# A recorded block of 7720 matmuls: the list scheduler's prices, array changes, clock, DMA rate and biases set anew

## The chip, the core and the metric

The kernel runs on one core of one Trainium2 chip. The metric is the time of one execution on the device in microseconds (us). PE is the matmul engine (TensorE), DVE, ACT and POOL are the vector, scalar and GpSimd engines, SP the queue that issues all the DMAs here.

## What is computed

One layer of a streaming encoder for 512 tokens of width 1024, in float32, with 16 learned tokens ahead of them (528 positions). Cut to what matters:

```python
u = rmsnorm(h); proj = u @ w_in                  # 1024 -> 8208 columns, cut into branches
c = c_val * sigmoid(c_gate)                      # conformer branch
c = causal_dwconv(c, 31 taps); c = silu(layernorm(c)); y_conf = c @ w_conf_out
q, k, v = silu(causal_dwconv(qkv, 4 taps))       # 8 heads of width 128; q, k normed
o = chunk_gated_delta_rule(q, k, v, g, beta)     # needs the inverse of a triangular matrix per chunk
y_dn = (rmsnorm(o) * silu(z)) @ w_dn_out
h = h + (sigmoid(gA) * y_conf + sigmoid(gB) * y_dn) @ w_out
f_gate, f_val = causal_dwconv(rmsnorm(h) @ w_up, 3 taps)   # 1024 -> 2 x 2816
out = rmsnorm(h + (silu(f_gate) * f_val) @ w_down)
```

## The kernel before, in words

**Products.** Features lie on partitions, tokens along the free dimension. A weight tile of 128 output columns (512 KB) is loaded by one DMA (`weights`), split into a rounded part `wh` (ACT) and the rest `wl` (DVE), and `gemm` multiplies it with an activation that is split in the same way: low weights by high activation, high by high, high by low. With 8 row blocks and two halves of the tokens (258 or 264 columns) that is 48 matmuls of the full 128x128 array to a tile; the text calls these **products** (`k`, `q`, `v`, `z` and `ga` are the branches of `w_in`, `cg` and `cv` the conformer's, then `y`, `wo`, `up`, `dn`).

**Small work.** The rest of PE's work uses a part of the array: the sums over partitions for the norms (`rs`: four matmuls of 128 rows and 32 columns for four groups of tokens, one on each group of 32 array columns, and all four in one PSUM bank), `ab` (32 columns of gates), the Gram matrices' corners (`ggm`, `qkm`), and the growing of the inverses from 32 to 128 rows (`gP`, `gX`: matmuls of 32x32 and 64x64, in `grow`). A stay of PE at such work, from the product before it to the product after it, is called a **visit** below. Transposes (`kt`, `vp`) are not counted as visits.

**What sets the order.** Nothing is issued directly. `record` writes the whole program down as calls (`Plan.add`), with the calls that each depends on. `Plan.price` gives each a duration. `Plan.order` then plays five engines against each other: at each step the engine that can start first takes, among its calls that are ready at that moment, the one with the lowest number. The number is the place in the program plus the biases of its stage (`BIAS`, `LNP`, `IVP`, `UP`, `WP`). `emit` hands the calls to the engines in that order, and each engine runs its own in sequence. So the numbers in the planner change no instruction; they change the order on each engine.

**What in it concerns PE.** A call that reads or adds to what another PE call wrote is ready 3 ns after it (`LAT['PE']['PE']`). For PSUM the place that a call touches is taken as its whole bank (`Vw.box`), so the four sums of one tile depend on each other in a row. In `look`, a call of the full array may not start before `drain`, which is 86 ns after the end of a small call, and `STAY` is added to its number while PE is at small work. The planner also keeps a model of PE's clock (`WIN`, `LOW`, `HIGH`).

Of the kernel before, what the change touches and what calls it, by code (L numbers as in the profile page):

```python
# [12 lines left out]
F32R = mybir.dt.float32r  # L13
# [53 lines left out]
class Vw:  # L67
    """a view of a tile: the steps to it, and the same steps taken on a stand-in to know its bounds"""
# [52 lines left out]
class Op:  # L121
    _fields = ("eng", "fn", "a", "k", "prio", "deps", "succ", "late", "wait", "cost", "ready", "end", "tiles", "lat", "table")
# [18 lines left out]
WIN = 3413.3  # L141
LOW = 0.4
HIGH = 0.84
# ---- the order: how far ahead of the first open call each engine looks, slots kept for the tile that is next in
# line, what it costs to leave a run of small products or to change a function table ----
AHEAD = {'PE': 3000, 'DVE': 3000, 'ACT': 3000, 'POOL': 400, 'SP': 400}
KEEP = {"p1": 1, "st": 1, "bt": 2}
STAY = 3000
SWITCH = 600
# [1 line left out]
BIAS = {'k3': -850, 'iv': -1500, 'd0': 150, 'v4': -30, 'v2': 0, 'd7': 1500, 'z1': -320, 't11': -280, 'z5': 0, 't7': 250, 'k0': -250, 'ln': 250, 's7': 30, 'z0': -700, 'o2': -250, 'o5': 100, 'd5': -1850, 'g3': 150, 'd6': -250, 'd1': 2130, 'k2': -30, 'q7': -1720, 'k5': -30, 's4': -730, 'd4': 850, 'w3': -1600, 't2': -600, 'c5': -130, 't8': 60, 'v3': 250, 'o4': -600, 'q6': -250, 'g4': -350, 't4': -100, 'o1': 250, 'q4': -630, 't9': -150, 'z2': -600, 'o0': -600, 'g0': 30, 'q3': 250, 'q5': 700, 'c1': 30, 'c6': -130, 's1': 0, 't15': 200, 't1': -700, 's3': 100, 'y0': 250, 't12': -150, 'o6': 100, 'o3': 250, 'k4': -100, 'w2': 250, 't5': -250, 'v0': 30}  # L151
LNP = 74
IVP = 1265
UP = 519
WP = 144
# [39 lines left out]
class Plan:  # L195
# [18 lines left out]
    def add(self, eng, fn, a, k):  # L214
        o = Op()
# [26 lines left out]
        o.part = eng == "PE" and fn == "matmul" and (writes[0].shape[0] < P or args[1].shape[0] < P) and writes[0].shape[0] % 32 == 0  # L242
        o.share = args[1].shape[0] / P if o.part else 1.0
        o.cost, o.lat = self.price(eng, fn, a, k, writes[0])
        if eng == "ACT" and fn == "activation":
            o.table = TABLES.get(str(k["func"]).split(".")[-1])
        self.ops.append(o)

    def price(self, eng, fn, a, k, out):
        n = out.n  # L250
        if eng == "PE":
            lhs, rhs = (k["lhsT"], k["rhs"]) if fn == "matmul" else (a[1], a[2])
            n = rhs.n
            if fn == "transpose":
                return 110, 0
            # a tile of the array beside one that is busy costs its issue alone
            if out.ap.offset // out.tl.row:
                return 22, 0
            return max(n, lhs.n) / 2.4 * (1 if lhs.tl.dt == F32R else 4) + 3, 0
        if fn == "dma_start":  # L260
            runs = [v.ap.ap[-1][1] if v.ap.ap[-1][0] == 1 else 1 for v in (k["out"], k["in_"])]
            return 475, int(np.prod(out.shape)) * 4 / 360.0 * (1 if min(runs) > 127 else 2)
# [10 lines left out]
    def order(self):  # L273
        """list scheduling: the engine that can start first takes its ready call of the lowest number"""
# [17 lines left out]
        part, drain = False, 0.0  # L292
        # a memset waits until the call that it is for has one other thing to wait for
# [13 lines left out]
        def look(e, t):  # L307
            """the call to take at t, or the next moment when there may be one"""
            q, nxt, best = ready[e], later[e][0][0] if later[e] else None, None
            for p, i in q:  # L310
# [23 lines left out]
                if e == "PE" and not o.part:  # L334
                    st = max(st, drain)
# [3 lines left out]
                if e == "PE" and part and not o.part:  # L339
                    p += STAY  # L340
                elif o.table and table not in o.table:
                    p += SWITCH
# [4 lines left out]
        while len(out) < len(ops):  # L347
# [26 lines left out]
            if e == "PE":  # L374
                # the tensor engine's clock: full after a busy window, half after an idle one
# [8 lines left out]
                act += c * o.share  # L384
                part, drain = o.part, t + c + 86 if o.part else 0.0
            free[e] = t + c
            o.end = free[e]
            if e == "SP":
                dma = max(dma, t + 1100) + o.lat
                o.end = dma + 950  # L390
# [4 lines left out]
            for v in o.tiles:  # L395
# [4 lines left out]
                if not v.left and v.tag in slots:  # L400
                    heapq.heappush(slots[v.tag], tend[v] + 100)
            for j in o.succ:
                s = ops[j]
                s.ready = max(s.ready, o.end + LAT[e][s.eng])
# [25 lines left out]
def record(A, out):  # L430
# [41 lines left out]
    def weights(src, n=D):  # L472
        """raw tile -> its 12-bit part and the exact rest"""
# [9 lines left out]
    def gemm(acc, ws, ah, al, ranges, k0=0, kn=None, first=True, last=True):  # L483
# [17 lines left out]
    def sums(ss, width):  # L501
        """tiles [128, width]: sum over tiles and partitions, four token groups on partition groups"""
# [8 lines left out]
    def spread(r, width, n):  # L511
        """such rows on every partition of a tile in SBUF"""
# [9 lines left out]
    def rstd_rows(ss, width, scale, bias):  # L522
        """the sums' 1/sqrt(scale*sum+bias)"""
# [19 lines left out]
    # the first products take the input without its norm's scale, which comes after them  # L543
# [3 lines left out]
    # products of nothing while the first loads run: the tensor engine's clock is up when they are in  # L547
# [34 lines left out]
    # 32 columns: four k-tiles at a time, side by side in the array; their sums come with the turn to tokens  # L582
# [38 lines left out]
    # halves of the products below come doubled out of (tanh + 1)  # L621
# [35 lines left out]
    # beta = exp(min(b, 0)) / (1 + exp(-|b|))  # L657
# [9 lines left out]
    # cumulated decays: by token on partitions, by row, and the chunks' totals  # L667
# [47 lines left out]
    def conv4(acc, t, way=None):  # L715
        """four causal taps, then silu; from PSUM [128, 2, 268], or [128, 2, 264] moved out first, or SBUF"""
# [37 lines left out]
    def decays(h):  # L754
        """E[j, i] = exp(gc_i - gc_j) for j <= i, else 0"""
# [9 lines left out]
    def grams(h):  # L765
# [23 lines left out]
        # b = beta / (|k|^2 + eps)  # L789
# [22 lines left out]
    def inverses():  # L812
# [15 lines left out]
        def steps(M, X, w, n, c0, c1):  # L828
            """X = (I - M)^-1 for strictly upper M, columns c0 to c1, last rows first"""
# [461 lines left out]
```

## Time and profile before

| | us |
|---|---|
| median of 3 runs | 1049.65 (1049.23 to 1053.68) |
| span of the profiled execution | 1049.7 |
| PE busy | 1035.5 |
| DVE busy | 718.3 |
| ACT busy | 474.7 |
| POOL busy | 9.5 |
| mean granted clock of PE | 0.985 |

The profiled execution was one of the same kernel, and its span of 1049.7 is the time of the median run to 0.1 us, so sums are made against 1049.7. Matmuls are pipelined and overlap in the records: the busy time of PE says that it always had something under way, not that it was at its best pace. What a matmul costs is therefore read from the starts of the ones that follow each other.

### The profile page before, as it was taken

To read this page: it belongs to the slowest core of one execution; us is meant where nothing else is said; L and a number is where in the kernel's file an instruction comes from. 1 tells how busy PE (TensorE), PEld (TensorE's weight loads), DVE (VectorE), ACT (ScalarE), POOL (GpSimd) and SP (SyncE) were. 2 spreads that over 40 slices of the span, in tenths; PEclk is the share of its full clock that TensorE was granted. 3 is DMA by queue.
4 is the path that set the end of the run, shared out by engine and by line. 5 is a ranking of instruction groups with operands and counts; after the bars stand their busy time and mean duration, and the time that the engine had idled before them with its cause. 6 is when DMAs were issued, how large, how long until landed. Compare 5 with 4: busy or idle time off the path is not lost.

```text
span 1049.7 us, 20033 instructions
## 1 busy us (share of the span) xinstructions
PE 1035.5 (99%) x8430; PEld 985.7 (94%) x8430; DVE 718.3 (68%) x1237; ACT 474.7 (45%) x863; POOL 9.5 (1%) x45
## 2 busy tenths in 40 slices
PE   9999999999999999999999999999999999999996
PEld 7999999988989999999999999999999999988885
DVE  6987899984867998985546555666666767623324
ACT  6777622557534466444345234534444443413222
POOL 0011000000000000000000000000000000000000
PEclk9999999987999999999999999999999999999998
DMA  6244323231211232212313343232323232333232
GB/s 223 76 123 110 114 82 111 81 102 42 71 42 61 81 106 98 78 65 76 127 61 122 101 143 99 81 102 81 100 81 101 81 101 81 96 91 91 81 105 81
DMA packets 44042, 98.40 MB, mean 94 GB/s; under 512 B 12720, under 2 KB 19248, under 8 KB 43952
## 3 DMA queue, kind: packets, MB, share of 16 engines
q1 hardware_dynamic: 43952, 97.12, 29.2%
q8 instruction: 66, 1.08, 0.4%
q14 instruction: 24, 0.20, 0.1%
HBM read 93.89 MB, written 3.21 MB: 93 GB/s over the span
## 4 chain that ended last, share of the span: by engine, by line
PE 96%; DVE 1%; ACT 1%; DMA 0%; SPq 0%; issue 0%; POOL 0%; DVEq 0%; POOLq 0%; ACTq 0%
PE up L427 24%; PE dn L427 12%; PE ga L427 9%; PE y L427 9%; PE k L427 5%; PE v L427 5%; PE z L427 5%; PE q L427 4%; PE wo L427 4%; PE cv L427 4%; PE cg L427 4%; PE rs L427 2%; PE o L427 2%; PE gX L427 1%; PE S L427 1%; PE gP L427 1%
## 5 line engine op out<-in xcount | busy, mean ns | idle before, releaser
L427 DVE TENSOR_TENSOR wl<-wr,wh 128x1024 fp32r<-128x1024 f32 x157 | 189.3, 1207 | 160.1 <-PE dn L427 47.8
L427 ACT CAST wh<-wr 128x1024 fp32r<-128x1024 f32 x157 | 162.0, 1037 | 287.5 <-PE up L427 87.8
L427 DVE SCALAR_TENSOR_TENSOR ca<-c,par,ca 128x516 f32<-128x516 f32 (+10 forms) x240 | 177.3, 744 | 7.3 <-ACT ca L427 4.8
L427 PE MATMUL up<-hl,wh 128*128 128x258 f32 x704 | 142.1, 283 | 0.0
L427 PE MATMUL up<-hh,wh 128*128 128x258 f32 x704 | 142.1, 283 | 0.0
L427 PEld LDWEIGHTS up<-hh,wh 128*128 128x128 f32 x704 | 109.0, 190 | 0.2 <-issue 0.2
L427 PEld LDWEIGHTS up<-hl,wh 128*128 128x128 f32 x704 | 108.9, 189 | 0.0
L427 PE MATMUL up<-hh,wl 128*128 128x258 f32 x704 | 92.4, 283 | 0.0
L427 PEld LDWEIGHTS up<-hh,wl 128*128 128x128 f32 x704 | 88.3, 189 | 0.0
L427 DVE TENSOR_TENSOR up<-up,r 128x258 f32<-128x258 f32 x88 | 33.4, 420 | 49.0 <-PE up L427 46.0
L427 DVE SCALAR_TENSOR_TENSOR uy<-up,par,uy 128x512 f32<-128x512 f32 x88 | 65.9, 748 | 1.5
L427 PE MATMUL dn<-fh,wh 128*128 128x512 f32 (+1 forms) x198 | 65.0, 369 | 0.0
L427 PE MATMUL dn<-fl,wh 128*128 128x512 f32 (+1 forms) x198 | 64.9, 369 | 0.0
L427 ACT ACTIVATE uy<-up,par 128x512 f32<-128x512 f32 x44 | 36.0, 817 | 53.8 <-DVE up L427 53.8
L427 PE MATMUL ga<-uh,wh 128*128 128x258 f32 x256 | 58.5, 290 | 0.0
L427 PE MATMUL ga<-ul,wh 128*128 128x258 f32 x256 | 57.9, 289 | 0.0
L427 DVE SCALAR_TENSOR_TENSOR cv<-ra,par,cv 128x528 f32<-128x528 f32 x69 | 51.6, 760 | 0.6 <-ACT cv L427 0.5
L427 PE MATMUL dn<-fh,wl 128*128 128x512 f32 (+1 forms) x198 | 49.8, 370 | 0.0
L427 PE MATMUL ga<-uh,wl 128*128 128x258 f32 x256 | 48.4, 299 | 0.0
L427 PEld LDWEIGHTS dn<-fh,wh 128*128 128x128 f32 x198 | 36.9, 188 | 7.8 <-ACT wh L427 1.2
L427 PEld LDWEIGHTS dn<-fl,wh 128*128 128x128 f32 x198 | 36.9, 188 | 6.9
L427 PEld LDWEIGHTS ga<-ul,wh 128*128 128x128 f32 x256 | 42.2, 189 | 0.8 <-issue 0.6
(284 smaller groups left out, 2238.9 us busy)
## 6 DMA issues: line engine op xcount, KB each, us to landing
wr<-in_win SPq DMA_DIRECT2D x64, 512.0 KB, 3.3
wr<-in_wup SPq DMA_DIRECT2D x44, 512.0 KB, 3.7
wr<-in_wd SPq DMA_DIRECT2D x17, 512.0 KB, 3.6
wr<-in_wdn SPq DMA_DIRECT2D x8, 512.0 KB, 3.2
wr<-in_wco SPq DMA_DIRECT2D x8, 512.0 KB, 3.4
wr<-in_wo SPq DMA_DIRECT2D x8, 512.0 KB, 3.3
wr<-in_wd SPq DMA_DIRECT2D x8, 384.0 KB, 3.1
x<-in_xT SPq DMA_DIRECT2D x8, 264.0 KB, 5.8
```

The lines of the kernel that those rows point to most:

```text
L427: getattr(engines[o.eng], o.fn)(*(get(x) for x in o.a), **{n: get(x) for n, x in o.k.items()})
```

## The change

The planner's numbers are replaced, and three rules of it. The calls recorded, their operands and their data do not change; the comments were dropped, so line numbers shift (L427 becomes L446). What is new:

- a product is priced by `RATE`, a 64-row product at 115, other plain float32 matmuls by their columns at 0.6 per ns; DMAs run at 310 bytes per ns and end after a `tail`;
- a small matmul has a `mode` (rows and columns of the array, rounded up); each change of mode on PE is charged by `TURN` (92, 105 or 190 ns); a successor on another engine waits 110 more after a small one;
- the rule that a full-array call may not start before `drain` is gone; `STAY` goes from 3000 to 6000 and is charged on every change of mode away from small work;
- the clock's model takes `LOW` = 0.5 and another measure of activity; `SWITCH` goes from 600 to 192;
- `BIAS`, `LNP`, `IVP` and `WP` get new values.

```diff
+RATE = 0.4453
+TURN = {(False, True): 92, (True, False): 105, (True, True): 190}
+LOW = 0.5
 HIGH = 0.84
...
-STAY = 3000
-SWITCH = 600
...
+STAY = 6000
+SWITCH = 192
...
+LNP = -756
+IVP = 1865
 UP = 519
-WP = 144
+WP = 114
...
-        o.part = eng == "PE" and fn == "matmul" and (writes[0].shape[0] < P or args[1].shape[0] < P) and writes[0].shape[0] % 32 == 0
-        o.share = args[1].shape[0] / P if o.part else 1.0
+        o.mode = None
+        if eng == "PE" and fn == "matmul":
+
+            up = lambda n: 32 if n <= 32 else 64 if n <= 64 else P
+            o.mode = (up(args[1].shape[0]), up(writes[0].shape[0]))
+            o.mode = None if o.mode == (P, P) else o.mode
         o.cost, o.lat = self.price(eng, fn, a, k, writes[0])
...
             if out.ap.offset // out.tl.row:
                 return 22, 0
-            return max(n, lhs.n) / 2.4 * (1 if lhs.tl.dt == F32R else 4) + 3, 0
+            if lhs.tl.dt == F32R:
+
+                return RATE * n + 4 + (2 if rhs.ap.offset % rhs.tl.row % 4 else 0), 0
+            if lhs.shape[0] == 64:
+                return 115, 0
+            return max(n, lhs.n) / 0.6 + 8, 0
...
-                if e == "PE" and not o.part:
-                    st = max(st, drain)
                 if st > t:
                     nxt = st if nxt is None else min(nxt, st)
                     continue
-                if e == "PE" and part and not o.part:
+                if e == "PE" and mode and o.mode != mode:
                     p += STAY
...
-                act += c * o.share
-                part, drain = o.part, t + c + 86 if o.part else 0.0
+                act += o.act * (2 if cold else 1)
+                if o.mode != mode:
+                    c += TURN[bool(mode), bool(o.mode)]
+                mode = o.mode
...
+            drain = 110 if o.mode else 0
             for j in o.succ:
                 s = ops[j]
-                s.ready = max(s.ready, o.end + LAT[e][s.eng])
+                s.ready = max(s.ready, o.end + LAT[e][s.eng] + (drain if s.eng != e else 0))
```

The order that comes out, at three places. All rows are of PE; a row names the tile that is written, the tiles read, and the output's shape; `sq` are squared input tiles, `hsel` and `ones` the sums' weights, `q` with `hsel` a squared query, `LL`, `mn`, `gp`, `p` and `DU` the parts of the inverses.

The sums for the first norm, some 15 us into the program, ahead of the products that finish the second key tile. Before:

```order
L427 MATMUL ab_206<-x_188,wab_123 32x264
L427 MATMUL ab_213<-x_188,wab_123 32x264
L427 MATMUL rs_192<-sq_281,ones_65 32x132 x4
L427 MATMUL rs_192<-sq_299,ones_65 32x132 x4
L427 MATMUL rs_192<-sq_312,ones_65 32x132 x4
L427 MATMUL k_185<-xl_309,wh_153 128x264 x2
```

After the change, the same sums:

```order
L446 MATMUL rs_192<-sq_291,ones_65 32x132
L446 MATMUL k_218<-xh_264,wh_200 128x264
L446 MATMUL rs_192<-sq_291,ones_65 32x132
L446 MATMUL k_218<-xh_264,wh_200 128x264
L446 MATMUL rs_192<-sq_291,ones_65 32x132
L446 MATMUL k_218<-xl_268,wh_200 128x264
L446 MATMUL rs_192<-sq_291,ones_65 32x132
L446 MATMUL k_218<-xl_268,wh_200 128x264
```

Three sets of four sums stood in one row of small work; now a product of the second key tile stands between any two sums.

The sums for the norm of heads 0 to 3, a third of the way through the program. Before, two sets of four stand together (the other sums of this tile alternate with the 32x32 matmuls of `gX`):

```order
L427 MATMUL z_4724<-uh_93,wh_4606 128x258 x2
L427 MATMUL z_4724<-ul_95,wh_4606 128x258
L427 MATMUL rs_3819<-o_4_4726,hsel_71 32x129 x4
L427 MATMUL rs_3819<-q_4_4314,hsel_71 32x129 x4
L427 MATMUL z_4724<-ul_95,wh_4606 128x258
L427 MATMUL z_4724<-uh_97,wh_4606 128x258 x2
```

After:

```order
L446 MATMUL v_4082<-uh_143,wl_4039 128x264
L446 MATMUL rs_3678<-o_2_3579,hsel_71 32x129
L446 MATMUL q_4170<-ul_115,wh_4091 128x264
L446 MATMUL rs_3678<-q_2_3236,hsel_71 32x129
L446 MATMUL q_4170<-ul_115,wh_4091 128x264
L446 MATMUL rs_3678<-q_2_3236,hsel_71 32x129
L446 MATMUL q_4170<-uh_119,wh_4091 128x264
```

Here too each sum now stands by itself between products of `v` and `q`.

The growing of the first inverses (`grow`), a fifth of the way through. Before:

```order
L427 MATMUL gP_4_3193<-LL_2950,mn_1279 64x64 x4
L427 MATMUL ga_2915<-uh_113,wl_2874 128x258
L427 MATMUL S_1_3201<-w_3188,kd_920 128x128
L427 MATMUL o_1_2764<-E_991,w_3188 128x128
L427 MATMUL ga_2915<-uh_117,wl_2874 128x258 x2
L427 MATMUL ga_2915<-uh_125,wl_2874 128x258 x2
```

After:

```order
L446 MATMUL gP_4_3265<-LL_2908,mn_1287 64x64
L446 MATMUL vp_3257<-cst_202,cv_2848 128x128
L446 MATMUL gP_4_3265<-LL_2908,mn_1287 64x64
L446 MATMUL ga_3121<-uh_127,wh_2870 128x258
L446 MATMUL wP_3273<-r_4_3263,mn_1107 128x128
L446 MATMUL gP_4_3265<-LL_2908,mn_1287 64x64
L446 MATMUL ga_3121<-ul_131,wh_2870 128x258
L446 MATMUL gP_4_3265<-LL_2908,mn_1287 64x64
L446 MATMUL ga_3121<-ul_131,wh_2870 128x258
```

The four 64x64 matmuls of one problem stood in one run, and are now spread over full-array work.

## Rows read from the trace of the kernel before

**Rows 1.** The page: busy time by engine, and the chain that ended last.

```profile
PE 1035.5 (99%) x8430; PEld 985.7 (94%) x8430; DVE 718.3 (68%) x1237; ACT 474.7 (45%) x863; POOL 9.5 (1%) x45
PE 96%; DVE 1%; ACT 1%; DMA 0%; SPq 0%; issue 0%; POOL 0%; DVEq 0%; POOLq 0%; ACTq 0%
```

**Rows 2.** The chain in order of time: start, us, what; its longest piece.

```profile
666.99 245.65 PE up L427 x2033
```

**Rows 3.** PE's timeline, 66 to 68 us: start, us, instruction, count of records.

```profile
66.11 0.41 PE L427 MATMUL gr<-cst,g__1_817 128*32 128x128 f32 x2
66.45 0.87 PE L427 MATMUL k<-uh,wl 128*128 128x268 f32 x5
67.25 0.20 PE L427 MATMUL grm<-cst,g__1_817 16*8 16x16 f32 x2
67.39 0.39 PE L427 MATMUL k<-uh,wl 128*128 128x268 f32 x1
67.70 0.21 PE L427 MATMUL ggm<-cv 128*16 128x16 f32 x2
```

**Rows 4.** PE's timeline at sums: four of a tile, then twelve.

```profile
455.02 0.28 PE L427 MATMUL z<-uh,wl 128*128 128x258 f32 x1
455.23 0.43 PE L427 MATMUL rs<-o,hsel 128*32 128x129 f32 x8
455.59 0.39 PE L427 MATMUL ga<-ul,wh 128*128 128x258 f32 x1
455.81 0.28 PE L427 MATMUL z<-uh,wl 128*128 128x258 f32 x1
...
538.11 0.87 PE L427 MATMUL rs<-sq,ones 128*32 128x129 f32 x24
...
539.14 0.40 PE L427 MATMUL y<-oh,wh 128*128 128x258 f32 x2
```

**Rows 5.** PE's timeline where small work of two shapes stands together.

```profile
464.60 0.43 PE L427 MATMUL rs<-o,hsel 128*32 128x129 f32 x8
464.95 0.39 PE L427 MATMUL w<-v,Tm 16*16 16x128 f32 x2
465.27 0.39 PE L427 MATMUL ga<-uh,wl 128*128 128x258 f32 x1
465.50 0.28 PE L427 MATMUL z<-uh,wh 128*128 128x258 f32 x1
```

**Rows 6.** The first norm's end, timeline of PE, ACT and DVE.

```profile
23.06 1.06 PE L427 MATMUL rc<-rr,cst 128*128 128x132 f32 x8
23.87 0.37 PE L427 MATMUL k<-xh,wh 128*128 128x264 f32 x1
23.93 0.66 ACT L427 COPY rx<-rc 128x264 f32<-128x264 f32 x2
24.81 0.70 DVE L427 TENSOR_TENSOR ra<-k,rx 128x528 f32<-128x528 f32 x1
```

**Rows 7.** Windows: length, busy PE, PEld, DVE, ACT, POOL (counts), granted clock, DMA.

```profile
225.00:250.00 25.00, 24.10 (x302) 21.66 (x302) 15.01 (x27) 18.26 (x56) 0.00 (x0) 0.73 0.17 54
250.00:275.00 25.00, 24.67 (x254) 22.82 (x252) 16.46 (x29) 15.63 (x44) 0.44 (x3) 0.86 0.15 44
...
225.00:230.00 5.00, 4.28 (x136) 3.66 (x135) 4.79 (x9) 4.65 (x20) 0.00 (x0) 1.00 0.25 78
230.00:235.00 5.00, 4.82 (x41) 3.90 (x42) 3.74 (x6) 2.26 (x9) 0.00 (x0) 0.56 0.08 30
...
290.00:295.00 5.00, 5.00 (x41) 3.10 (x40) 2.91 (x5) 1.58 (x6) 0.00 (x0) 1.00 0.12 48
```

**Rows 8.** Waits of PE, whole run: engine, tile, releaser, us in total, times, longest.

```profile
PE rb L427 <- DVE rr L427: 3.1, 1, 3.1
PE gg L427 <- ACT kd L427: 2.0, 2, 1.2
```

**Rows 9.** ACT's group of table loads: count, busy us, mean ns, idle before.

```profile
L427 ACT ACT_TABLE_LOAD x22 | 28.2, 1283 | 1.1 <-PEq L1283 0.7
```

More of the change, by code (lines that the diff above doesn't have):

```diff
@@ L121 @@
 class Op:
-    _fields = ("eng", "fn", "a", "k", "prio", "deps", "succ", "late", "wait", "cost", "ready", "end", "tiles", "lat", "table")
+    _fields = ("eng", "fn", "a", "k", "prio", "deps", "succ", "late", "wait", "cost", "ready", "end", "tiles", "lat", "table", "mode", "act", "tail")
 class Rec:
@@ L141 @@
 WIN = 3413.3
-LOW = 0.4
+RATE = 0.4453
+TURN = {(False, True): 92, (True, False): 105, (True, True): 190}
+LOW = 0.5
 HIGH = 0.84
@@ L147 @@
 KEEP = {"p1": 1, "st": 1, "bt": 2}
-STAY = 3000
-SWITCH = 600
-BIAS = {'k3': -850, 'iv': -1500, 'd0': 150, 'v4': -30, 'v2': 0, 'd7': 1500, 'z1': -320, 't11': -280, 'z5': 0, 't7': 250, 'k0': -250, 'ln': 250, 's7': 30, 'z0': -700, 'o2': -250, 'o5': 100, 'd5': -1850, 'g3': 150, 'd6': -250, 'd1': 2130, 'k2': -30, 'q7': -1720, 'k5': -30, 's4': -730, 'd4': 850, 'w3': -1600, 't2': -600, 'c5': -130, 't8': 60, 'v3': 250, 'o4': -600, 'q6': -250, 'g4': -350, 't4': -100, 'o1': 250, 'q4': -630, 't9': -150, 'z2': -600, 'o0': -600, 'g0': 30, 'q3': 250, 'q5': 700, 'c1': 30, 'c6': -130, 's1': 0, 't15': 200, 't1': -700, 's3': 100, 'y0': 250, 't12': -150, 'o6': 100, 'o3': 250, 'k4': -100, 'w2': 250, 't5': -250, 'v0': 30}
-LNP = 74
-IVP = 1265
+STAY = 6000
+SWITCH = 192
+BIAS = {'k3': -4130, 'iv': -2610, 'd0': -1790, 'v4': -70, 'd7': -250, 'z1': -490, 't11': 100, 't7': 850, 'k0': -2740, 'ln': 3280, 's7': -320, 'z0': -700, 'o2': 900, 'o5': 600, 'd5': 90, 'g3': 600, 'd6': -320, 'd1': 3350, 'k2': -120, 'q7': -1720, 's4': -210, 'd4': 1120, 'w3': -1320, 't2': -600, 't8': 30, 'v3': 150, 'o4': -470, 'g4': -350, 't4': -250, 'o1': 570, 'q4': -630, 't9': -250, 'z2': 30, 'o0': 100, 'q3': 250, 'q5': 700, 'c1': -30, 'c6': -30, 's1': -100, 't15': 200, 't1': -920, 's3': 70, 'y0': 250, 't12': -620, 'o6': -1250, 'o3': 1230, 'w2': 250, 't5': -220, 'v0': -160, 't13': 30, 'g7': -30, 'q1': -220, 'k1': 350, 't14': 570, 'y2': 100, 'c3': -2450, 'z6': 280, 'm3': -30, 'w5': 160, 'd2': 480, 'd3': 160, 'c2': 130, 's5': -1470, 's6': 250, 'v5': 600, 'w1': 40, 'm1': 30, 't3': 30, 'm7': 100, 'y3': 370, 'w0': -100, 'y7': 30, 'y6': 30, 'v6': -30, 'g6': -30, 'g1': 170, 'o7': -250, 'm2': 30, 'z4': -30, 'w6': 1500, 'c4': 130, 't0': 570, 'w7': -30}
+LNP = -756
+IVP = 1865
 UP = 519
-WP = 144
+WP = 114
 WARM = 16
@@ L241, in add @@
         o.deps, o.succ, o.table = deps, [], None
-        o.part = eng == "PE" and fn == "matmul" and (writes[0].shape[0] < P or args[1].shape[0] < P) and writes[0].shape[0] % 32 == 0
-        o.share = args[1].shape[0] / P if o.part else 1.0
+        o.mode = None
[3 more added lines that the diff above has]
+            o.mode = None if o.mode == (P, P) else o.mode
         o.cost, o.lat = self.price(eng, fn, a, k, writes[0])
+        o.act = (args[2].n if writes[0] is args[0] else args[1].n) / 0.6 * o.mode[0] / P if o.mode else o.cost
+        o.tail = 950 + (1500 if fn == "dma_start" and o.lat > 700 and self.run(k) <= P else 0)
         if eng == "ACT" and fn == "activation":
@@ L247, in add, with run @@
         self.ops.append(o)
+    @staticmethod
+    def run(k):
+        return min(v.ap.ap[-1][1] if v.ap.ap[-1][0] == 1 else 1 for v in (k["out"], k["in_"]))
     def price(self, eng, fn, a, k, out):
@@ L258, in price @@
                 return 22, 0
-            return max(n, lhs.n) / 2.4 * (1 if lhs.tl.dt == F32R else 4) + 3, 0
+            if lhs.tl.dt == F32R:
[3 more added lines that the diff above has]
+            return max(n, lhs.n) / 0.6 + 8, 0
         if fn == "dma_start":
-            runs = [v.ap.ap[-1][1] if v.ap.ap[-1][0] == 1 else 1 for v in (k["out"], k["in_"])]
-            return 475, int(np.prod(out.shape)) * 4 / 360.0 * (1 if min(runs) > 127 else 2)
+            return 475, int(np.prod(out.shape)) * 4 / 310.0 * (1 if self.run(k) >= P else 2)
         aps = sum(isinstance(k.get(x), Vw) for x in ("scalar", "scalar1", "scalar2", "scale", "bias", "mul"))
@@ L291, in order @@
         win, act, cold = 0, 0.0, True
-        part, drain = False, 0.0
+        mode = None
         for i, o in enumerate(ops):
@@ L388, in order @@
             if e == "SP":
-                dma = max(dma, t + 1100) + o.lat
-                o.end = dma + 950
+                dma = max(dma, t + 950) + o.lat
+                o.end = dma + o.tail
             out.append(i)
```

## The prediction

> **What bounds the kernel now.** First the page: PE is busy 99% of the span, and the chain that ended last is 96% PE [rows 1]. That says only that PE never lacks work, so the next thing to read is the pace. In the chain's longest piece 2033 products follow each other in 245.65 us, 0.121 us each [rows 2]; a product of 264 columns takes 0.122 by the same reading. No reordering makes these shorter. So the time is the sum of PE's work in sequence, plus what PE loses: to small work between products, to a lower clock, and to waits. These three I look for in the timeline, the windows and the waits, in that order.
>
> *Small work.* From the start of `grm` to the start of `ggm` are 0.45 us, and only one product lies between [rows 3]. So a visit whose own streaming is nearly nothing (16 columns) costs 0.45 - 0.12 = **0.33 us**. From `gr` to `grm` are 1.14 us with five products (0.61): 0.53 for a single matmul of 128 rows, 32 columns of the array and 128 streamed, the very shape of a lone sum [rows 3]. Four sums of a tile cost hardly more: from the product before them at 455.02 to the second one after them at 455.81 are 0.79 us with two products, so 0.55 [rows 4]. Twelve sums take 1.03 from their start to the second product, against 0.58 for four: 0.22 for each further four [rows 4]. So a set of sums streams for 0.22, whether one stands there or four side by side, and each visit adds **0.32** whatever is in it. Going from one small shape to another costs less: sums and `w` together take 0.90 to the second product where sums alone take 0.58, and of the 0.32 more, 0.21 are w's own 128 columns, like a sum's; 0.11 is the change [rows 4, 5].
>
> *Clock.* The granted clock is 0.73 in 225 to 250 us and 0.86 in 250 to 275, so between its two levels 6.75 and 3.5 us of the high clock's time, **10.2 us** together, are lost there [rows 7]. It fell when `grow`'s small matmuls had PE nearly to themselves: 136 matmuls in 225 to 230, and 0.56 in the next window [rows 7].
>
> *Waits.* PE's named waits are the last norm's (3.1) and 2.0 for `kd` near 105 us [rows 8].
>
> Priced so (products by pace, other float32 matmuls by their columns, 0.32 a visit, 0.1 a change of shape), the order of before gives 1025 us; the other 25 are 3.4 at the start, 2.4 near 105, some 9 in 225 to 275, and 11 at the end.
>
> **The change, part by part.** It alters no instruction, so every term is a matter of order. I counted visits in both built orders: **69 before, 164 after**; changes between small shapes inside a visit: 58 before, 13 after. The reason is in the code. The next sum of a bank is ready 3 ns after the one before it. While `drain` stood, no product could start for 86 ns, and the sum went first. Without `drain` the product can start at once, the sum 3 ns later cannot yet be chosen, and `STAY` weighs only what is ready. So a product goes between, and every chain of small matmuls in one bank is torn apart.
>
> - *First norm.* 28 visits in place of 5, most around one sum: 23 x 0.32 = 7.4. The sums' streaming goes from 8 sets of four (1.8) to 25 sets (5.5), `ab` from 5.7 to 4.8: +2.8. Together **+10.2**. The inputs' arrival might hide a part of it, but most lone sums stand behind the last input's squares. Worse, both key tiles are now finished before `rc`. In before, products ran on from 23.87 while `rx` was copied and `ra` freed the first tile, done at 25.51, 1.4 us after the last `rc` [rows 6]; that cover is gone and the third tile waits: **+1.5**.
> - *Norm of heads 0 to 3.* In all head sums, 32 visits for 4: +28 x 0.32 = 9.0, 23 changes of shape fewer: -2.4, and 7 more streamed sets: +1.5. **+8.1.**
> - *Growing the inverses.* 58 visits for 16, 23 changes fewer: 13.4 - 2.4 = **+11.0.** A lone 32x32 or 64x64 visit does not occur before; its nearest rows are `grm` and `ggm` at 0.33, so 0.32 stands; I allow 0.05 either way, since neither is of these shapes.
> - *Second and last norm.* 10 visits for 4, and 1.0 of streaming: **+2.9.** The rest of the small work: -0.6.
> - *Waits near 105 us.* A later PE leaves ACT more time: 0 to -2.4, I take **-1.0**.
> - *The end.* The last twelve matmuls on PE stand as before; 0.
> - *Other engines and SP.* DVE is busy 68%, ACT 45% [rows 1]. Two more table loads, and moved casts and loads, lie under PE's work, which only gets longer; cost 0. If that cover were gone, a table load would cost its own 1.3 us [rows 9].
> - *Clock.* The growing of the first heads, 43 us of work by these prices, now mixes small matmuls and products one by one, hardly ever more than four full-array matmuls in a row. The ends: the clock holds (0, and the 10.2 of before come back), or it is low throughout. At the low clock before, work of 7.9 us by my prices took 13.65 (230.6 to 244.3), 1.72 times. 43 x 0.72 = 31 is the upper end. Before, it fell 5 us into such work; full-array work runs together again for over 1 us some 33 us into the stretch. So I take 28 us at 0.72: a loss of **20**, and 20 - 10.2 = +9.8 net. The window 290 to 295 warns against more: there too small work fills PE, yet with many sums in it, and the clock stayed 1.00 [rows 7]. So I expect no fall at the lone sums.
>
> Sum against the profiled execution, whose 1049.7 is also the median: 1049.7 + 10.2 + 1.5 + 8.1 + 11.0 + 2.9 - 0.6 - 1.0 + 9.8 = **1091.6 us**.
>
> **Rivals.**
>
> 1. *The clock holds.* The many products in the stretch keep it up. Then 1091.6 - 20 = **1071.6**. For it: the window 290 to 295 [rows 7]. Against it: 225 to 235, where PE was busy 4.28 and 4.82 of 5 us and the clock fell all the same [rows 7]. The Trainium skill, page "TensorE: Matmul & The Clock Gate", section "HAM oscillation — how this bites in real kernels", puts the low clock down to gaps in which the engine idles between bursts. By that rule the new order, which leaves no such gap, keeps the high clock, and this rival would be right; the trace disagrees, with a fall at 96% busy.
> 2. *Low throughout.* 1091.6 + 11 = **1102.6**, if full-array work in pieces of 1 to 2 us doesn't bring the clock back.
> 3. *Visits overlap with products.* If the small matmul runs beside the products around it, only fewer changes of shape (45 x 0.1 = 4.7), the clock (10.2) and the wait (2.4) are left: 1049.7 - 17.3 = **1032**, faster. It decides at a visit's price: 95 more visits and some 6 us more streaming eat 17.3 us from 0.12 us a visit on. Against it: 0.33 where a visit stands alone between two products [rows 3].
> 4. *No net change.* Cheap visits and a held clock could meet near 1050; it needs 0.12 to 0.2 us a visit, for which no row speaks.
>
> **How the numbers follow.** Forecast 0.50, rival 1 0.23, rival 2 0.19, rival 3 0.05, rival 4 0.03. The range goes from rival 1 with visits at the lower bound (95 x 0.05 = 5 less), **1066**, to rival 2 with 3 us of further falls, **1106**. Half a per cent is about what a measurement of this kernel can tell from no change: faster 0.05, same 0.03, slower 0.92.
>
> **What would show it.** In the profile of after: `rc` near 35 us in place of 23.06; a product between any two `rs` records at 15 to 35 us and again near 340 to 370, 0.65 us from sum to sum with one product between; then the first `up` product near 695 us (655.8 before), with no new idle time on PE; and a granted clock of 0.5 for some 50 us from about 230 on. PE busy would stay near 99%: the page's share can't show this loss. The forecast is wrong if visits between single products cost far under 0.3 us (`rc` below 28 us), or if the clock at 230 to 290 reads 1.00.

## The result, and the profile after

The changed kernel takes **1103.01 us** (1097.32 to 1113.23, four runs) against 1049.44 of the kernel before in the same comparison: a ratio of 1.0515, with an interval of 1.0453 to 1.0577. It is 5% slower. The profiled execution is the shortest of the four, 1097.32 us with a span of 1095.5. The four times follow the mean granted clock of TensorE: 0.980, 0.975, 0.971 and 0.963 for 1097.32, 1100.71, 1105.30 and 1113.23.

The page after, the lines that answer to [rows 1], and the longest piece of the chain in order of time (start, us, what), as in [rows 2]:

```profile
PE 1076.3 (98%) x8430; PEld 1001.0 (91%) x8430; DVE 717.0 (65%) x1237; ACT 477.8 (44%) x865; POOL 9.2 (1%) x45
PE 81%; DVE 11%; DMA 3%; ACT 2%; issue 1%; SPq 1%; POOL 0%; DVEq 0%; POOLq 0%; ACTq 0%
```

```profile
710.98 246.47 PE up L446 x2034
```

The chain now names DVE for 11%, but DVE is no busier than before and PE is idle for 19.2 us in all, so no other engine has become the bound. The same 8430 matmuls keep PE busy for 40.8 us more (1035.5 before); its idle time was 14.2. The pace of products has not changed: 2034 in 246.47 us, 0.121 us each. So it is again small work, clock and waits that must account for the difference.

PE's timeline of after (start, us, instruction, count of records; a plain float32 matmul makes two records, so x2 is one matmul), at the sums of the first norm, then at the end of that norm (with ACT and DVE), as in [rows 6]:

```profile
26.27 0.41 PE L446 MATMUL rs<-sq,ones 128*32 128x132 f32 x2
26.61 0.39 PE L446 MATMUL k<-xl,wh 128*128 128x264 f32 x1
26.93 0.41 PE L446 MATMUL rs<-sq,ones 128*32 128x132 f32 x2
...
37.69 1.06 PE L446 MATMUL rc<-rr,cst 128*128 128x132 f32 x8
38.56 0.66 ACT L446 COPY rx<-rc 128x264 f32<-128x264 f32 x2 [1.56 <-PE rc L446]
39.43 0.70 DVE L446 TENSOR_TENSOR ra<-k,rx 128x528 f32<-128x528 f32 x1
39.57 0.40 PE L446 MATMUL abp<-cst,abT 128*128 128x16 f32 x2 [0.82 <-DVE abT L446]
40.18 0.39 PE L446 MATMUL k<-xh,wh 128*128 128x264 f32 x1 [0.22 <-DVE ra L446]
```

From one sum to the next are 0.66 us with one product between, so 0.66 - 0.12 = 0.54 for a lone sum, the price that [rows 3] gave (0.53). `rc` starts at 37.69 in place of 23.06. Behind it stands what was ready: nothing but `abp` at 39.57, and the third key tile at 40.18.

The sums for the norm of heads 0 to 3, and lone matmuls of 64x64 and of 32x32 in the growing of the inverses, all at a granted clock of 1.00; last, four of 64x64 in one run in the kernel before:

```profile
353.51 0.41 PE L446 MATMUL rs<-q,hsel 128*32 128x129 f32 x2
353.85 0.39 PE L446 MATMUL q<-ul,wh 128*128 128x264 f32 x1
354.08 0.28 PE L446 MATMUL v<-uh,wl 128*128 128x264 f32 x1
354.29 0.41 PE L446 MATMUL rs<-o,hsel 128*32 128x129 f32 x2
```

```profile
284.87 0.32 PE L446 MATMUL gP<-LL,mn 64*64 64x64 f32 x2
285.12 0.39 PE L446 MATMUL q<-uh,wh 128*128 128x264 f32 x1
285.44 0.33 PE L446 MATMUL gP<-LL,mn 64*64 64x64 f32 x2
```

```profile
281.89 0.37 PE L446 MATMUL q<-uh,wh 128*128 128x264 f32 x1
282.19 0.24 PE L446 MATMUL gX<-DU,gp 32*32 32x32 f32 x2
282.36 0.39 PE L446 MATMUL ga<-uh,wh 128*128 128x258 f32 x1
282.68 0.22 PE L446 MATMUL gX<-DU,gp 32*32 32x32 f32 x2
```

```profile
229.07 0.68 PE L427 MATMUL gP<-LL,mn 64*64 64x64 f32 x8
```

Head sums: 0.78 with two products, 0.54 each. A lone 64x64 visit: 0.57 - 0.12 = 0.45. A lone 32x32 visit: 282.68 - 282.19 = 0.49, less 0.12, 0.37. Alone, the last two shapes had no row in the trace of before. In the run of four each further 64x64 matmul adds (0.68 - 0.32) / 3 = 0.12, so of the 0.45 some 0.33 are the visit and 0.12 the matmul's own columns, which cost as much inside a chain.

Windows of after (length, busy PE, PEld, DVE, ACT, POOL with counts, granted clock, DMA share, GB/s); the first four answer to [rows 7]:

```profile
225.00:250.00 25.00, 24.00 (x263) 20.66 (x261) 19.89 (x31) 18.43 (x58) 0.00 (x0) 0.79 0.32 65
250.00:275.00 25.00, 25.00 (x113) 18.48 (x112) 13.40 (x24) 7.24 (x21) 0.00 (x0) 0.53 0.15 44
235.00:240.00 5.00, 4.17 (x97) 2.94 (x96) 4.88 (x10) 4.76 (x19) 0.00 (x0) 0.95 0.02 3
240.00:245.00 5.00, 4.83 (x28) 4.02 (x26) 3.66 (x5) 4.80 (x15) 0.00 (x0) 0.50 0.00 0
...
75.00:125.00 50.00, 46.62 (x373) 43.74 (x372) 37.40 (x100) 38.20 (x135) 6.02 (x10) 1.00 0.45 130
525.00:575.00 50.00, 48.68 (x441) 47.30 (x440) 24.05 (x32) 22.69 (x33) 0.00 (x0) 1.00 0.31 97
```

The clock was lower for longer: by the reading of [rows 7], 5.25 and 11.75 us of the high clock's time are lost in 225 to 275, 17.0 against 10.2 before. It fell just ahead of 240, behind the window with 97 matmuls (before, behind the one with 136). The last two windows have a comparison in the kernel before, the same view:

```profile
75.00:125.00 50.00, 47.90 (x392) 46.19 (x391) 40.37 (x106) 36.35 (x131) 5.78 (x9) 1.00 0.41 106
525.00:575.00 50.00, 50.00 (x456) 48.58 (x456) 30.29 (x43) 27.37 (x40) 0.00 (x0) 1.00 0.29 96
```

PE's idle time near 105 us went from 2.1 to 3.4 (in the first 50 us, by the same view, from 1.1 to 2.3), and at the `y` products, where it had none, 1.3 are new. PE's named waits after (engine, tile, releaser, us in total, times, longest), as in [rows 8]:

```profile
PE rb L446 <- DVE rr L446: 2.9, 1, 2.9
PE ggm L446 <- ACT kd L446: 1.2, 1, 1.2
PE kt L446 <- DVE mn L446: 1.2, 1, 1.2
...
PE y L446 <- ACT wh L446: 0.7, 1, 0.7
PE y L446 <- DVE wl L446: 0.5, 1, 0.5
```

### The profile page after: what moved, and what is told of

Same layout as the page of the kernel before. It is cut to its first block, busy times and chain, and to the rows that moved or that the text cites. A ratio compares the mean times of both kernels' runs of the same rounds, so it can differ in the third digit from the quotient of the medians.

```text
span 1095.5 us, 20036 instructions
## 1 busy us (share of the span) xinstructions
PE 1076.3 (98%) x8430; PEld 1001.0 (91%) x8430; DVE 717.0 (65%) x1237; ACT 477.8 (44%) x865; POOL 9.2 (1%) x45
## 4 chain that ended last, share of the span: by engine, by line
PE 81%; DVE 11%; DMA 3%; ACT 2%; issue 1%; SPq 1%; POOL 0%; DVEq 0%; POOLq 0%; ACTq 0%
PE up L446 23%; PE dn L446 11%; PE ga L446 9%; PE y L446 7%; PE z L446 4%; PE wo L446 4%; PE v L446 4%; PE q L446 4%; DVE ca L446 3%; PE rs L446 2%; PE k L446 2%; DVE wl L446 2%; PE o L446 2%; DVE cv L446 1%; PE gX L446 1%
## 5 line engine op out<-in xcount | busy, mean ns | idle before, releaser
L446 DVE TENSOR_TENSOR wl<-wr,wh 128x1024 fp32r<-128x1024 f32 x157 | 189.4, 1207 | 189.6 <-issue 52.1
L446 ACT CAST wh<-wr 128x1024 fp32r<-128x1024 f32 x157 | 161.6, 1034 | 258.6 <-PE dn L446 61.1
L446 DVE SCALAR_TENSOR_TENSOR ca<-c,par,ca 128x516 f32<-128x516 f32 (+12 forms) x240 | 175.8, 743 | 2.5
L446 PE MATMUL up<-hl,wh 128*128 128x258 f32 x704 | 143.2, 285 | 0.0
L446 PE MATMUL up<-hh,wh 128*128 128x258 f32 x704 | 143.0, 284 | 0.0
L446 PEld LDWEIGHTS up<-hl,wh 128*128 128x128 f32 x704 | 109.7, 189 | 0.4 <-issue 0.4
L446 PEld LDWEIGHTS up<-hh,wh 128*128 128x128 f32 x704 | 109.5, 190 | 0.4 <-issue 0.4
L446 PE MATMUL up<-hh,wl 128*128 128x258 f32 x704 | 91.9, 282 | 0.0
L446 PEld LDWEIGHTS up<-hh,wl 128*128 128x128 f32 x704 | 87.7, 189 | 0.0
L446 DVE SCALAR_TENSOR_TENSOR uy<-up,par,uy 128x512 f32<-128x512 f32 x88 | 66.0, 749 | 1.5
L446 DVE TENSOR_TENSOR up<-up,r 128x258 f32<-128x258 f32 x88 | 33.5, 421 | 49.5 <-PE up L446 46.2
L446 PE MATMUL dn<-fh,wh 128*128 128x512 f32 (+1 forms) x198 | 65.4, 371 | 0.2 <-DVE xr L446 0.2
L446 PE MATMUL dn<-fl,wh 128*128 128x512 f32 (+1 forms) x198 | 64.9, 369 | 0.0
L446 PE MATMUL ga<-uh,wh 128*128 128x258 f32 x256 | 61.4, 302 | 0.8 <-DVE XT L446 0.8
L446 ACT ACTIVATE uy<-up,par 128x512 f32<-128x512 f32 x44 | 36.0, 817 | 59.2 <-DVE up L446 59.2
L446 PE MATMUL ga<-ul,wh 128*128 128x258 f32 x256 | 61.0, 300 | 0.0
L446 DVE SCALAR_TENSOR_TENSOR cv<-ra,par,cv 128x528 f32<-128x528 f32 x69 | 51.9, 762 | 0.7 <-ACT cv L446 0.6
L446 PE MATMUL dn<-fh,wl 128*128 128x512 f32 (+1 forms) x198 | 49.5, 369 | 0.0
L446 PEld LDWEIGHTS ga<-uh,wh 128*128 128x128 f32 x256 | 43.0, 193 | 3.1 <-issue 2.0
L446 PEld LDWEIGHTS ga<-ul,wh 128*128 128x128 f32 x256 | 43.1, 193 | 1.4 <-issue 0.4
L446 PEld LDWEIGHTS dn<-fh,wh 128*128 128x128 f32 x198 | 36.8, 188 | 8.1 <-ACT wh L446 1.3
L446 PEld LDWEIGHTS dn<-fl,wh 128*128 128x128 f32 x198 | 36.8, 188 | 6.9
```

What stands on the lines that cost most here:

```text
L446: getattr(engines[o.eng], o.fn)(*(get(x) for x in o.a), **{n: get(x) for n, x in o.k.items()})
```

## The experiments

The theory on trial (A) is that of the prediction: without the `drain` rule chains of small matmuls are torn apart, each visit costs 0.32 us beside its stream, and the clock falls for longer. Against it stand B, the new durations and biases themselves cost the time, and C, visits are cheap. The kernels, with the readings of one profiled execution each (vis1 and vis16 follow below). The ratio is to runs of before on the same chip (medians of 1046.0 to 1049.6) and is estimated from all runs, so it need not be the quotient of two medians; idle is span less PE busy; visits are counted in the traces, and agree with those of the built orders but for nobar, where 224 were expected:

| kernel | median us | ratio to before (interval) | span | PE busy | PE idle | visits |
|---|---|---|---|---|---|---|
| before | 1049.4 | | 1049.7 | 1035.5 | 14.2 | 69 |
| after | 1103.0 | 1.0515 (1.0453 to 1.0577) | 1095.5 | 1076.3 | 19.2 | 164 |
| bar | 1062.9 | 1.0127 (1.0104 to 1.0151) | 1062.6 | 1036.9 | 25.7 | 61 |
| lat0 | 1051.7 | 1.0032 (1.0008 to 1.0056) | 1051.8 | 1034.5 | 17.3 | 75 |
| lat0_turn | 1050.8 | 1.0011 (0.9995 to 1.0027) | 1048.8 | 1028.2 | 20.6 | 68 |
| nobar | 1137.2 | 1.0835 (1.0800 to 1.0870) | 1136.5 | 1120.4 | 16.1 | 210 |
| bar_rs | 1095.4 | 1.0440 (1.0371 to 1.0509) | 1099.5 | 1077.0 | 22.5 | 130 |
| newbias | 1060.0 | 1.0124 (1.0093 to 1.0154) | 1058.5 | 1038.7 | 19.8 | 72 |
| oldbias_bar | 1055.2 | 1.0091 (1.0071 to 1.0112) | 1051.7 | 1035.2 | 16.5 | 65 |
| refit_a | 1038.4 | 0.9892 (0.9857 to 0.9927) | 1037.8 | 1023.5 | 14.3 | 61 |
| refit_b | 1046.2 | 0.9976 (0.9953 to 1.0000) | 1041.6 | 1021.5 | 20.1 | 62 |
| refit_c | 1045.5 | 0.9956 (0.9941 to 0.9972) | 1044.7 | 1027.1 | 17.6 | 67 |

The time of one kernel moves with the granted clock from run to run: before took 1043.9 us at a mean clock of 0.996 and 1052.8 at 0.984. Where medians are only some us apart, runs of like mean clock are compared below.

**The rule put back in after (bar), and taken out of before (nobar).**

```diff
 bar, against after, in look() and order()
+                if e == "PE" and not o.mode:
+                    st = max(st, bar)
...
-                mode = o.mode
+                mode, bar = o.mode, t + c + 86 if o.mode else 0.0

 nobar, against before, in look()
-                if e == "PE" and not o.part:
-                    st = max(st, drain)
```

> The changed kernel with one thing put back: after a matmul on part of the array, no full-array call is placed for 86 ns, so that the next sum of a chain comes ahead of it. Durations, biases and every other number stay those of after. In the built order the visits (stretches of part-array work between full-array calls) fall from 164 to 61, the changes of small shape from 13 to 36. Theory A (torn chains, each visit 0.32 us, and the low clock under the spread sums): TensorE work priced by the rates of the prediction falls from 1056.5 to 1016.8 us, with the 25 us of waits and clock of before it gives 1042 us (1032 to 1050), and the last of the first norm's four scale transposes is done near 23 us instead of 37.7. Rival B (the new durations and biases, not the order inside the chains, cost the time): it stays at 1090 to 1105 us. Rival C (a visit overlaps with the products beside it): it stays within 5 us of after.

> The kernel before with the one thing taken out: the two lines that hold full-array calls back behind a matmul on part of the array. All durations, biases and array changes stay those of before. Visits 69 to 224, changes of small shape 58 to 85. Theory A: priced TensorE work rises from 1024.9 to 1095.1 us; with 25 to 45 us of waits and clock 1120 to 1140 us, slower than after, since here the planner's old numbers leave more chains torn. Rival B (the new durations and biases cost the time): it stays at 1045 to 1055 us. Rival C (visits overlap): within 10 us of before.

Two lines taken out of before cost 88 us (1137.2, A's 1120 to 1140), and put back in after they bring 40 of the 54 us back (1062.9). `rc` is at 22.03 in bar. B and C fall: with every old duration in place the loss is there, with every new one in place and the rule back most of it is gone. (bar counts every small matmul; before counted those whose output has 32 rows or a multiple.) But bar misses A's 1042 by 21 us. The pages of nobar and of bar, and bar's longest waits of PE:

```profile
PE 1120.4 (99%) x8430; PEld 1025.5 (90%) x8430; DVE 719.6 (63%) x1237; ACT 476.7 (42%) x864; POOL 8.8 (1%) x45
```

```profile
PE 1036.9 (98%) x8430; PEld 986.9 (93%) x8430; DVE 716.2 (67%) x1237; ACT 479.1 (45%) x865; POOL 8.3 (1%) x45
```

```profile
PE y L447 <- DVE gt L447: 3.8, 3, 1.5
PE rb L447 <- DVE rr L447: 3.3, 2, 3.1
PE kt L447 <- ACT kdm L447: 1.6, 1, 1.6
PE y L447 <- ACT gt L447: 1.5, 1, 1.5
```

In bar PE is as busy as before (1036.9 against 1035.5), so nearly all of the busy time that the torn chains cost is gone; what keeps it 13 us slower is mostly 11.5 us more of idle time, 5.3 of them `y` behind `gt`. I had taken the waits over from before, and the order of ACT and DVE is new too. That is 11.5 of the 21. The other 9.5 are busy time, which my prices put 8 us under that of before and which came out 1.4 above it; 3.5 of them are the clock by the windows (0.66 and 0.86 in 225 to 275, 0.93 in 525 to 550), and the rest stays open.

**Another repair of the same place (lat0, lat0_turn).** If the tear comes from the 3 ns between two sums, it must heal without any waiting rule when they are 0.

```diff
 lat0, against after
-LAT = {'PE': {'PE': 3, 'DVE': 200, 'ACT': 200, 'POOL': 200, 'SP': 200},
+LAT = {'PE': {'PE': 0, 'DVE': 200, 'ACT': 200, 'POOL': 200, 'SP': 200},

 lat0_turn, besides
-TURN = {(False, True): 92, (True, False): 105, (True, True): 190}
+TURN = {(False, True): 100, (True, False): 220, (True, True): 105}
```

> The changed kernel with another repair of the same place: the planner counts the next matmul of one PSUM bank as ready at once (0 ns) instead of 3 ns after the one before it. Nothing else differs from after, and no wait is put back. Visits 164 to 75, changes of small shape 13 to 4. Theory A: priced TensorE work 1016.1 us, with the 25 us of before 1041 us (1032 to 1050); the four scale transposes of the first norm are done near 23 to 24 us. Rival B (new durations and biases cost the time): 1090 to 1105 us. Rival C (visits overlap): within 5 us of after.

> The changed kernel with the 0 ns of the run beside it and array changes of 100 ns into a small matmul, 220 ns out of one and 105 ns between two small shapes, in place of 92, 105 and 190. Visits 68, changes of small shape 3, priced TensorE work 1013.5 us. Theory A: 1038 us (1028 to 1048), 2 to 4 us under the run with 0 ns alone and some 11 us under before. Rival B: 1090 to 1105 us. Rival C (visits overlap): no difference from the run with 0 ns alone.

One digit gives 51 us back: 1051.7, just above the 1050 that A allowed (1041 was its likeliest). So the mechanism is the one named: the next sum was 3 ns late for the choice.

The new charges for array changes show no gain. PE's busy time is 6 us less in lat0_turn (1028.2 against 1034.5), but the profiled executions had mean clocks of 0.988 and 0.981. That is 15 us less at the low level, and by the 0.4 us for each that bar_rs gives below, those 6 us. The medians are 0.9 apart; at a mean clock of 0.987 lat0 took 1048.4 and 1050.3, lat0_turn 1050.9 and 1051.2. A's 2 to 4 us are not there, and 1050.8 lies above its 1028 to 1048: the 11 us under before didn't come (1.0011).

**The price of a visit by itself (vis1, vis16).** One more lone matmul of 128 rows and 32 columns in each of the 44 `up` steps, between two products:

```diff
 vis1, against before, in up(); vis16 has 16 for P as the number of columns
+        vt = p1("vis")
+        PE.matmul(vt[:32, :P], lhsT=ones[:, :32], rhs=u[:, :P], start=True, stop=True)
```

> The kernel before, with the disputed cost added by itself: in each of the 44 steps of the gated feed-forward's first stage one more matmul of 128 rows into 32 columns of the array, 128 data columns, which only reads the finished u and whose result nobody uses. The planner puts each between two products. Theory A (a visit has a fixed cost of 0.32 us beside its own stream of 0.22): 44 x 0.53 = 23 us more than before, 1073 us (1068 to 1078). Rival C (a visit overlaps with the products beside it): at most 44 x 0.1 = 4 us more, 1050 to 1054 us.

> As the run with 44 lone matmuls added, with 16 data columns in place of 128, so that the stream is almost nothing and the fixed part of a visit is left. Theory A: 44 x 0.33 = 14.5 us more than before, 1064 us (1059 to 1069), and some 9 us less than with 128 columns. If the whole cost were the stream: 1050 to 1053 us.

The medians are 1073.4 (a ratio of 1.0252, 1.0196 to 1.0308) and 1066.2 (1.0190, 1.0169 to 1.0211) against 1046.0 of before: 27 and 20 us more, in place of 23 and 14.5. The stage shows the price without the clock's scatter. The instructions of the tile `up` in before, vis1 and vis16 (count, duration in ns, first and last start in us; the last ones of the stage, and `vis`):

```profile
L427 PE MATMUL up<-hh,wh x704: 279/283/385, 655.8 to 910.2; 128*128 128x258 f32 x176
L427 PE MATMUL up<-hh,wl x704: 277/283/290, 660.2 to 912.3; 128*128 128x258 f32 x176
```

```profile
L427 PE MATMUL up<-hh,wh x704: 279/283/385, 655.9 to 933.6; 128*128 128x258 f32 x176
L427 PE MATMUL up<-hh,wl x704: 277/282/388, 660.3 to 935.7; 128*128 128x258 f32 x176
L427 PE MATMUL vis<-up,ones x88: 272/285/297, 668.4 to 937.0; 128*32 128x128 f32 x88
```

```profile
L427 PE MATMUL up<-hh,wh x704: 278/283/385, 651.6 to 921.2; 128*128 128x258 f32 x176
L427 PE MATMUL up<-hh,wl x704: 277/283/387, 655.9 to 923.4; 128*128 128x258 f32 x176
```

From the first `up` product to the last are 256.5 us in before, 279.8 in vis1, 271.8 in vis16. 43 of the 44 visits lie in that stretch, so a visit costs 23.3 / 43 = 0.54 us with 128 data columns and 15.3 / 43 = 0.36 with 16. The difference of 0.18 is the stream of 112 columns, and 0.33 are left for a visit without any. C falls here too. The few us by which the medians go beyond the stage come with the clock: the runs of before beside them had mean clocks of 0.987 to 0.994, vis1 0.983 to 0.996 and vis16 0.986 to 0.991; at 0.990 vis1 took 1071.28 and before 1046.88, 24.4 apart.

**The growing alone left torn (bar_rs).** The rule put back behind `rs` and `ab` only:

```diff
 bar_rs, against bar
-                mode, bar = o.mode, t + c + 86 if o.mode else 0.0
+                mode, bar = o.mode, t + c + 86 if o.mode and any(v.name in ('rs', 'ab') for v in o.tiles) else 0.0
```

> The changed kernel with the wait restored behind the norms' sums and the two small gate columns' matmuls (rs, ab) only; the chains that grow the inverses (gP, gX) stay torn. Visits 130 in place of 164 (61 with the wait everywhere), priced TensorE work 1041.9 us in place of 1056.5 (1016.8). Theory A: the norms' part is worth 15 us and a little waiting comes back, so 1085 to 1092 us, and the granted clock in 225 to 275 us stays as low as in after, 30 us or more at 0.5. If the growing were cheap (a visit of 32x32 or 64x64 matmuls far under 0.32 us): within 5 us of the run with the whole wait, 1060 to 1068 us.

It took 1095.4 us: two runs at 1089.2 and 1089.4 with a mean clock of 0.978, two at 1101.3 and 1102.0 with 0.964 and 0.963, above A's 1085 to 1092. So 32 us of the distance to bar (1062.9) come from the growing. The norms' part, put at 15, is 8 by the medians; at a mean clock of 0.963 after took 1113.2 and bar_rs 1102.0, 11 apart. The windows of the profiled execution, one of the longer ones, and the first of them in bar:

```profile
225.00:250.00 25.00, 24.65 (x126) 18.67 (x124) 12.45 (x20) 11.52 (x35) 0.00 (x0) 0.51 0.06 20
250.00:275.00 25.00, 25.00 (x131) 18.89 (x130) 13.57 (x22) 8.36 (x25) 0.34 (x2) 0.50 0.09 33
275.00:300.00 25.00, 25.00 (x156) 21.00 (x157) 14.05 (x23) 7.30 (x18) 0.10 (x1) 0.63 0.00 1
```

```profile
225.00:250.00 25.00, 23.27 (x214) 19.14 (x214) 20.91 (x36) 16.65 (x54) 0.00 (x0) 0.66 0.11 37
```

A clock of 0.51, 0.50 and 0.63 means 68 us at the low level, all in the stretch where 32x32 and 64x64 matmuls alternate with single products. With the growing whole, bar has 0.66 and 0.86 in the first two of these windows and 1.00 in the third: the torn growing is what keeps the clock low, and for how long differs between runs of one program. The mean clocks say what it costs: 0.964 over 1099.5 us are 79 us at the low level, 0.978 over 1087 are 48, and the times are some 12 apart, so some 0.4 us for each us at the low clock.

**Whose waits are they? (newbias, oldbias_bar, and biases fitted anew.)** bar has new durations and new biases. Against the theory that the biases bring its waits (A') stand D, the new durations bring them, and E, the new durations are a gain and only the new biases cost time. Each alone, with the rule in place:

```diff
 newbias, against before (the table BIAS of after as well)
-LNP = 74
-IVP = 1265
+LNP = -756
+IVP = 1865
...
-WP = 144
+WP = 114

 oldbias_bar, against bar: the same the other way round
```

> The kernel before with the new table of biases and the three new offsets (LNP, IVP, WP) alone; durations, array changes and the wait behind small matmuls stay those of before. Visits 72 in place of 69, priced TensorE work 1024.3 us in place of 1024.9. Theory A': the 13 us by which the changed kernel with the wait restored stays above before are waits of TensorE (its idle time there is 25.7 us, before 14.2), and they come from biases that were set for another order: then here too the waits grow, 1055 to 1065 us. Rival D (the new durations bring them): 1046 to 1052 us here.

> The changed kernel (new durations, array changes, clock, DMA rate) with the wait behind small matmuls restored and the biases and offsets of before. Visits 65, priced TensorE work 1017.6 us, about that of the run with the wait alone restored (1016.8). Theory A' (biases that fit another order bring the waits): the old biases do not fit these durations either, so no better than 1063 us, or worse. Rival D (the new durations bring the waits): 1058 to 1068 us. Rival E (new durations do what they are meant to, only the new biases cost time): 1040 to 1049 us, faster than before.

The new biases alone cost before 14 us (1060.0 against 1046.0; some 10 at a mean clock of 0.987, 1059.8 and 1060.3 against 1049.5), with 5.6 us more idle time (19.8 against 14.2); D fails there. The old biases with the new durations give 1055.2, which none of the three expectations held: 9 us slower than before, 8 faster than with the new biases. Most of the 9 goes with the clock: oldbias_bar's four runs had 0.983 to 0.985, those of before beside it 0.987 to 0.994; at 0.984 it took 1054.2 and 1056.2, and before, in the runs beside the other kernels, 1051.8 to 1052.8, 3 us less. So with the rule in place the new biases cost some 10 us with either durations, and the new durations some 3. That the new biases suffer from durations they weren't found with isn't shown.

Biases found anew for the repaired numbers should then bring the waits down. refit_a and refit_b start from the biases of before, refit_c from those of after; the rest is lat0_turn:

> The changed kernel with 0 ns from sum to sum and the array changes of the run lat0_turn (100, 220, 105), and its biases and offsets fitted anew to these numbers, starting from those of before. Visits 61, changes of small shape 3, priced TensorE work 1011.3 us (lat0_turn 1013.5, before 1024.9). Theory A' (chains whole, and biases that fit the order keep the waits small): idle time of TensorE near the 14 us of before in place of 20.6, so 1036 to 1046 us, faster than both kernels. Rival D (the new durations bring the waits, whatever the biases): 1047 to 1055 us.

> As refit_a, another set of biases found from the same start: visits 62, changes of small shape 5, priced work 1011.8 us. Theory A': 1037 to 1047 us. Rival D: 1047 to 1055 us.

> As refit_a, with biases fitted from the start of those of after: visits 67, changes of small shape 3, priced work 1013.2 us. Theory A': 1038 to 1049 us, at least as fast as lat0_turn (1050.8). Rival D: 1047 to 1055 us.

They took 1038.4 (0.9892, 0.9857 to 0.9927), 1046.2 (0.9976, 0.9953 to 1.0000) and 1045.5 us (0.9956, 0.9941 to 0.9972). refit_a is faster than both kernels, 11 us under before and 65 under after. Its page:

```profile
PE 1023.5 (99%) x8430; PEld 980.9 (95%) x8430; DVE 718.0 (69%) x1237; ACT 477.5 (46%) x864; POOL 8.7 (1%) x45
```

12 us less of PE's time than before, and idle time back at 14.3. So the new durations bring no waits that biases can't take away (D falls): with the same numbers, biases alone are worth 12 us (lat0_turn 1050.8), in the other two sets 5. Those two lie within half a per cent of before, with idle times of 20.1 and 17.6, so a search doesn't always bring the waits down. Whether the old durations would do as well with biases searched for as long wasn't tried.

## Why the prediction was right or wrong

The direction, the cause and the range held (1066 to 1106; measured 1103.0); the likeliest value, 1091.6, was 11.4 us short. That splits into three parts. The sum was made on a span: 1091.6 stands against the 1095.5 of the profiled execution, **3.9 short**. All runs that list both have a time 1.7 to 1.9 us above the span (1097.32 and 1095.5 here), and that the span of before equalled the median of its runs was chance; I left these **1.8** out. And the profiled execution had the highest clock of the four; the median is **5.7** above it.

- *Small work: right in price, 2 to 4 us short in sum.* Predicted 31.6 us for 95 more visits and their streams (10.2 + 8.1 + 11.0 + 2.9 - 0.6). A lone sum measures 0.54 in after and 0.54 in vis1, 0.36 for 16 columns, against 0.53 and 0.33 by [rows 3]. `rc` is at 37.69 (near 35 predicted), `up` at 698.3 (695), a product stands between the sums in both norms. With the clock's term PE's busy time was to rise by 41.4 us; it rose by 40.8. That close fit is in part luck: if 5.7 to 6.8 of it are the clock's (below), 34 to 35 are left for small work, and two misses cancel. Where these 2 to 4 us lie stays open.
- *The growth's price: right.* 0.32 was taken over from other shapes, 0.05 allowed. A lone 32x32 visit is 0.37 and a lone 64x64 one 0.45. Their own columns are 0.05 (at the 1.6 ns a column of vis1 and vis16) and 0.12, spent in a chain as well; 0.32 and 0.33 are left.
- *The clock: right in kind, sized too high for this execution.* By one reading of the windows 17.0 us are lost against 10.2, so +6.8 where +9.8 was predicted; it fell about 9 us later than put, and stayed low 34 us where some 50 were expected. The forecast mixed two measures: its 20 is 28 us of work that take 48 at the low level, 0.42 us lost for each of these; its 10.2 counts 0.5 for each. At 0.42 for both, before lost 8.6, the forecast is +11.4, and this execution has +5.7. Over the runs it is otherwise: a mean clock of 0.971 over 1103.5 us is 64 us at the low level, the tail behind the last products included. The forecast lay between the executions, and rival 2 (1102.6) describes the longer ones.
- *Rival 1, the clock holds: fell.* In 250 to 275 PE was busy 25.00 of 25 us, at a granted clock of 0.53 in after and 0.50 in bar_rs. The Trainium skill, page "TensorE: Matmul & The Clock Gate", section "HAM oscillation — how this bites in real kernels", ties the low clock to idle gaps between bursts. By that rule the clock would have held there; the trace disagrees, as it did before the change.
- *The waits near 105 us: wrong sign.* The step was that a later PE leaves ACT more time, -1.0. Idle time in 75 to 125 rose from 2.1 to 3.4. ACT's and DVE's own order was changed by the same numbers, and what PE waits for there (`kd`, `mn`) came later still; which of the numbers did that isn't shown.
- *No new idle time: wrong.* 1.3 us in 525 to 575, where `y` waits for its split weights. Idle time rose by 5.0 in all (1.2 of it in the first 50 us, where the third key tile waits), and the sum had the tile's +1.5 and the -1.0, so 0.5. These 4.5 us are the short part of the span's sum; the busy time was off by 0.6 the other way.
- *Cost nothing on the other engines: half right.* DVE is no busier (717.0), ACT by 3.1 us (477.8), and what was moved on them delayed nothing for long in after. In bar, where PE reaches the same places earlier, it is idle for 25.7 us in place of 19.2, which suggests that a part of that cover was the lost time itself.

## What to carry to other kernels

A list scheduler chooses among what is ready at that instant. A latency of 3 ns inside a chain, too small to matter by itself, decides whether the chain stays whole, and a penalty for leaving weighs nothing against work that isn't ready. Ahead of taking out a rule that looks like a crude wait, count in the built order what it holds together.

Here biases alone made 12 us between two kernels with the same durations. Whoever corrects the durations of a planner should search its priorities again, and look for the new waits as well as for the work saved.

## What the runs showed of the hardware that was not expected

The price of a visit was read ahead of the change; the runs add that it holds by itself. A switch of TensorE from full-array products to a lone small matmul and back costs 0.33 us with next to no data (vis16), and the busy share doesn't tell (98 to 99% in every kernel here).

One program's clock can stay at its low level for quite different times: 79 us in one execution of bar_rs and 48 in another, by their mean clocks.

In nobar the clock fell again in the growing of later heads, where lone 32x32 and 64x64 matmuls alternate with other work. Two windows, and PE's timeline about the second fall, where a `gX` goes from 0.24 to 0.31 us:

```profile
325.00:350.00 25.00, 25.00 (x186) 23.47 (x186) 17.09 (x29) 9.06 (x23) 0.10 (x1) 0.86 0.07 26
375.00:400.00 25.00, 25.00 (x181) 22.93 (x180) 21.67 (x30) 11.50 (x21) 0.13 (x2) 0.89 0.24 85
```

```profile
393.37 0.24 PE L425 MATMUL gX<-DU,gp 32*32 32x32 f32 x2
393.54 0.38 PE L425 MATMUL ga<-uh,wh 128*128 128x258 f32 x1
...
395.02 0.31 PE L425 MATMUL gX<-DU,gp 32*32 32x32 f32 x2
395.27 0.47 PE L425 MATMUL vp<-cst,cv 128*128 128x128 f32 x1
```

The same kind of work stood at a clock of 1.00 in after, at 281 to 286 us. At lone sums, of which nobar has many as well, no fall is seen: none of its `rs` records lasts longer than 0.30 us, as long as those of after at a clock of 1.00.
